# A two-layer MoE block and a two-layer FFN block on one core: the branch around the general path moved in front of the last group's third product

## The chip, the cores and the metric

The kernel runs on one core of one Trainium2 chip. The metric is device time in microseconds (us), here a median of several executions. A profile is one execution taken by the hardware profiler. The core's engines each work through their own queue of instructions in order: TensorE (PE; PEld are its weight loads), VectorE (DVE), ScalarE (ACT), GpSimd (POOL) and SyncE (SP), whose queue issues all loads here. They wait for each other by semaphores.

## The reference, cut to what matters

Two blocks run one after the other on 256 tokens of width 1024. The first has two layers of mixer and mixture of experts (MoE); the second has two layers of FFN, mixer, FFN. The change is in the MoE, which runs once per layer of the first block, and at its seam with what comes next:

```python
def run_block(args):                 # for each block of 128 assigned tokens
    tok, g, e = args
    xb = h2[tok]
    y = (jax.nn.silu(xb @ w1[e]) * (xb @ w3[e])) @ w2[e]
    return y * g[:, None]
...
    x = x + g2 * ffn                 # ffn: the sum of the experts' outputs of a token
```

Each token goes to two of sixteen experts. After the MoE of layer 0 comes `h = rms_norm(x, ...) * (1 + sc1) + sh1` and `proj = h @ in_w` of the odd mixer; after that of layer 1 comes `rms_norm_2(x, ...)` and `h @ w_gate` of the first FFN of the second block. So the stage behind needs the complete x.

## The kernel before, in words

The MoE packs the sixteen experts into seven groups of two or four experts (GROUPS), each of at most 128 rows of tokens in all, so that a group's tokens stand on the 128 partitions. For a group there are three products: the first with w1 and the second with w3 (line 1100, `up`), and the third with w2 (line 1119, `down`). Between them ScalarE applies silu (line 1162), VectorE multiplies by the second product and the gate (line 1169, tile hm), TensorE transposes hm (line 1106) and ScalarE copies the transposed tile out of PSUM (line 1108, tile tf), which is the third product's stationary operand. Behind it `weigh` scales by g2 (line 1128, tile yg) and splits the result into two parts (lines 301 and 303, tile yp), and `combine` multiplies by the transposed one-hot matrix ohT (lines 1136 and 1137) and adds to x (line 1138). The third product and the combine of a group run during the first two products of the next one. At the end of the loop the last group's third product (the function `finish`) and its combine stand alone.

An expert may receive more tokens than its place in a group holds. For those there is a general path (`overflow`, line 1208 on): a flag is loaded from SBUF into a register of each engine (line 1210), each engine compares and branches (line 1211, `tc.If`), and the body handles two blocks of 64 tokens at a time, up to four times. With the inputs measured the flag is zero, and the body is jumped over. At the join behind the body each engine waits until what it had issued before the branch is done, and then raises its semaphores by what the body would have raised them; SyncE waits for all its loads there.

Weights come in loads of 1 MB (line 266, tile raw, ten buffers; some as two halves through line 279 into the buffers wH and wL). They are issued by SyncE in program order, each when its buffer is free. For the dense products a load is split into two tiles of half the mantissa: ScalarE rounds it into wH (line 301), and VectorE or GpSimd writes the rest into wL (line 303). `ahead_of` runs at the end of the MoE: for the next stage's first two loads (`unit`, od_in in layer 0, the first FFN's gate weights in layer 1), it issues the load alone ("raw", layer 0) or the load and the split (False, layer 1).

The order of instructions on each engine is not the source's. The tile framework places each instruction by its own estimates, within what dependences and buffers allow, so a split of line 301 that the source writes in the next stage can stand ahead of the branch. What order results is shown below for the places that matter.

The next stage begins with `take` for each half of x: squares for the norm (line 448 on ScalarE, 450 on VectorE), and in layer 1 transposes of x (line 492) and their split into xTH and xTL (lines 495 and 496), which the FFN's products read (lines 321 to 323). In layer 0 x is first normed (xn, lines 464 and 465), then transposed (line 476) and split into hH and hL (lines 609 and 610) for the products of lines 562 to 564.

## Time and profile before

| | us |
|---|---|
| median of 3 runs | 1807.15 |
| lowest, highest | 1804.95, 1808.47 |
| the profiled execution's own time | 1807.92 |
| its span, first to last instruction | 1805.7 |
| TensorE busy in it | 1715.2 (95%) |
| VectorE, ScalarE, GpSimd busy | 904.5, 719.0, 96.2 |
| mean granted clock of TensorE, of full speed | 0.982 |

The span lies 2.2 us below the execution's own time. TensorE is busy for 95% of it, so the places of interest are those where it isn't. Two of them are the ends of the two MoE layers, at 439 to 461 us and at 805 to 835 us of the span, where the last group's third product and combine are done, the branch is passed, and the next stage's input is made. In timelines a row that ends in "[8.95 <-PEq L1211]" was preceded by 8.95 us of idle time on its engine, which ended with what stands behind the arrow; a "q" marks an engine's sequencer, which runs branches and semaphore waits.

### The profile page before, as it was taken

The numbers are of one execution on the slowest core, as the hardware profiler recorded it, in microseconds if no ns is written. First come the engines' busy times: TensorE is split into PE (matmuls) and PEld (weight loads), VectorE is DVE, ScalarE is ACT, GpSimd is POOL, SyncE is SP. The second block draws the span as 40 slices with busy tenths as digits, with TensorE's granted clock in tenths as the row PEclk, the third lists the DMA queues.
The fourth block names the chain that finished last, engine by engine and source line by source line (L and its number), as shares of the span: only waits on it lengthen the run. The fifth ranks groups of instructions, "written<-read, shape, count | busy, mean of one in ns | idle before, by whom it ended". The sixth has DMA issues, their size and how long they took to land.

```text
span 1805.7 us, 23867 instructions
## 1 busy us (share of the span) xinstructions
PE 1715.2 (95%) x9320; PEld 1202.5 (67%) x9320; DVE 904.5 (50%) x1570; ACT 719.0 (40%) x1100; POOL 96.2 (5%) x138
## 2 busy tenths in 40 slices
PE   6899999998899999997999999999999999999998
PEld 4765633333766433335888888888888888888886
DVE  3893632213657412125555665555465546655554
ACT  2434411111473211104444666544354436664442
POOL 0580000000100000000000000000000000000000
PEclk9899999999899999998999999999999999999999
DMA  9946699999977999997655642654655555426530
GB/s 365 354 165 256 247 404 418 417 415 381 339 281 267 356 412 417 416 411 271 198 187 180 198 158 94 209 182 169 194 180 185 186 187 203 141 94 210 186 117 24
DMA packets 148652, 454.81 MB, mean 252 GB/s; under 512 B 8608, under 2 KB 18992, under 8 KB 130608
## 3 DMA queue, kind: packets, MB, share of 16 engines
q1 hardware_dynamic: 148528, 453.16, 68.1%
q8 instruction: 78, 1.28, 0.3%
q14 instruction: 46, 0.38, 0.1%
HBM read 452.07 MB, written 1.05 MB: 251 GB/s over the span
## 4 chain that ended last, share of the span: by engine, by line
PE 53%; ACT 1%; issue 0%; DVE 0%; POOL 0%; DVEq 0%; POOLq 0%; ACTq 0%
PE acc L321 16%; PE acc L322 16%; PE acc L323 16%; PE tp L1293 1%; PE acc L1446 1%; PE tp L492 1%; PE acc L1356 1%; PE tp L1440 0%; PE tp L1410 0%; ACT wH L301 0%; PE acc L1385 0%; PE acc L1350 0%; ACT t L448 0%; PE acc L1351 0%; PE acc L1352 0%
## 5 line engine op out<-in xcount | busy, mean ns | idle before, releaser
L303 DVE TENSOR_TENSOR wL<-raw,wH 128x1024 fp32r<-128x1024 f32 x369 | 450.5, 1226 | 407.0 <-ACT wH L301 406.4
L301 ACT ACTIVATE wH<-raw 128x1024 fp32r<-128x1024 f32 x372 | 391.1, 1059 | 425.6 <-PE acc L323 393.4
L321 PE MATMUL acc<-wH,xTH 128*128 128x512 f32 (+1 forms) x928 | 353.0, 381 | 0.1
L323 PE MATMUL acc<-wH,xTL 128*128 128x512 f32 (+1 forms) x928 | 347.8, 377 | 2.4 <-DVE xTL L496 2.4
L322 PE MATMUL acc<-wL,xTH 128*128 128x512 f32 (+1 forms) x928 | 348.7, 377 | 0.0
L323 PEld LDWEIGHTS acc<-wH,xTL 128*128 128x128 f32 x928 | 174.4, 188 | 37.4 <-DVE xTL L496 3.7
L1100 PE MATMUL acc<-raw,xg 128*32 128x512 f32 (+1 forms) x1088 | 195.2, 596 | 3.8 <-DMA raw<-in_ex_w_dram 3.8
L321 PEld LDWEIGHTS acc<-wH,xTH 128*128 128x128 f32 x928 | 174.8, 188 | 32.1 <-ACT xTH L495 1.0
L322 PEld LDWEIGHTS acc<-wL,xTH 128*128 128x128 f32 x928 | 174.8, 188 | 32.1
L322 PE MATMUL acc<-wL,tH 128*128 128x512 f32 x352 | 139.2, 395 | 0.0
L321 PE MATMUL acc<-wH,tH 128*128 128x512 f32 x352 | 138.4, 393 | 0.0
L323 PE MATMUL acc<-wH,tL 128*128 128x512 f32 x352 | 137.4, 390 | 0.0
L1100 PEld LDWEIGHTS acc<-raw,xg 128*32 128x32 f32 (+1 forms) x1088 | 53.7, 120 | 115.1 <-issue 105.0
L1119 PE MATMUL acc<-raw,tf 128*64 128x512 f32 (+1 forms) x320 | 86.0, 599 | 1.1 <-DMA raw<-in_ex_w_dram 1.1
L365 PE MATMUL acc<-raw,condb 128*32 128x256 f32 x768 | 72.4, 494 | 9.9 <-DMA raw<-in_mod_w_dram 9.9
L562 PE MATMUL acc<-hH,wH 128*128 128x256 f32 x256 | 76.3, 298 | 5.7 <-ACT wH L301 5.7
L1169 DVE SCALAR_TENSOR_TENSOR hm<-acc,gg,hm 128x512 f32<-128x512 f32 x14 | 15.4, 1102 | 128.9 <-PE acc L1100 128.9
L335 POOL TENSOR_TENSOR rs<-ms,mhalf 128x1 f32<-128x1 f32 x22 | 12.1, 553 | 1252.9 <-DVE ms L334 1238.8
L1128 DVE TENSOR_TENSOR yg<-acc,g 128x512 f32<-128x512 f32 x28 | 19.2, 691 | 114.0 <-PE acc L1119 100.2
L321 PEld LDWEIGHTS acc<-wH,tH 128*128 128x128 f32 x352 | 66.1, 188 | 14.9
L323 PEld LDWEIGHTS acc<-wH,tL 128*128 128x128 f32 x352 | 66.1, 188 | 14.3
L563 PE MATMUL acc<-hL,wH 128*128 128x256 f32 x256 | 74.5, 292 | 0.8 <-DVE hL L610 0.8
(366 smaller groups left out, 2218.3 us busy)
## 6 DMA issues: line engine op xcount, KB each, us to landing
raw<-in_ex_w_dram SPq DMA_DIRECT2D x140, 1024.0 KB, 15.0
raw<-in_ffn_w_gate_dram SPq DMA_DIRECT2D x44, 1024.0 KB, 5.1
raw<-in_ffn_w_up_dram SPq DMA_DIRECT2D x44, 1024.0 KB, 5.1
raw<-in_ffn_w_down_dram SPq DMA_DIRECT2D x44, 1024.0 KB, 4.8
raw<-in_mod_w_dram SPq DMA_DIRECT2D x64, 512.0 KB, 7.9
rawwH<-in_ex_w_dram SPq DMA_DIRECT2D x52, 512.0 KB, 13.8
rawwL<-in_ex_w_dram SPq DMA_DIRECT2D x52, 512.0 KB, 12.6
raw<-in_w_in_dram SPq DMA_DIRECT2D x20, 1024.0 KB, 5.1
```

The lines of the kernel that those rows point to most:

```text
L301: S.activation(H, src, AF.Copy)
L303: eng.tensor_tensor(L, src, H.bitcast(F32), op=OP.subtract)
L321: TE.matmul(o, aH, bH, start=start, stop=False)
L322: TE.matmul(o, aH, bL, start=False, stop=False)
L323: return TE.matmul(o, aL, bH, start=False, stop=stop)
L365: TE.matmul(ps[32 * i:32 * i + 32, :], condb[:, k, :], quarter(raw[:, k % 2], i), start=k == 0, stop=k == 7)
L492: TE.transpose(ps[:, j, :], src[:, j * P:(j + 1) * P], ident)
L562: TE.matmul(o, ws[kk][0][:, cs], hH[:, k, :], start=k == 0 and c % 2 == 0, stop=False)
L563: TE.matmul(o, ws[kk][0][:, cs], hL[:, k, :], start=False, stop=False)
L1100: TE.matmul(ps[c:c + w, :], xg[:, k, c:c + w], ws[e][j], start=k == 0, stop=k == 7)
L1119: TE.matmul(y[h][c:c + w, :], tf[:, k, c:c + w], ws[e][j][:, half(h)], start=k == 0, stop=k == 3)
L1128: V.tensor_mul(yg, y[h], g2[:, half(h)])
```

## The change

At the end of the MoE's loop, the combine of the group before the last now comes first; then the loads of the last group's w2 are issued, then `ahead_of` and the branch, and only behind the branch stand the last group's transposed tile, its third product and its combine (`finish`). As the last group's tiles now have to outlive the general path, that has tiles of its own: `hmo` for hm, one buffer `one` of 128x512 for the weights (two of 128x1024 before, kept; now each use loads a half anew), and ohT has five buffers in place of four. In layer 1 `ahead_of` only loads, as in layer 0; the splits are then made where the first FFN asks for them, which gives wL of its first two loads to GpSimd (`FLEAD = 2`). The lines behind the first edit move by one (1211 becomes 1212, 301 becomes 302).

```diff
--- before.py
+++ after.py
@@ -283,15 +283,16 @@
     class Singly:
 
 
-        def __init__(self, ap, pl):
-            self.ap, self.pl, self.held = ap, pl, {}
-
-        def __getitem__(self, j):
-            if j not in self.held:
-                v = self.pl.tile([P, 1024], F32, name="one", bufs=2)[:, :self.ap.shape[2]]
-                nc.sync.dma_start(v, self.ap[:, j, :])
-                self.held[j] = v
-            return self.held[j]
+        def __init__(self, ap, pl, j=None):
+            self.ap, self.pl, self.j = ap, pl, j
+
+        def __getitem__(self, at):
+            if self.j is None and self.ap.shape[2] > 512:
+                return type(self)(self.ap, self.pl, at)
+            j, cols_ = (at, slice(0, 512)) if self.j is None else (self.j, at[1])
+            v = self.pl.tile([P, 512], F32, name="one", bufs=1)
+            nc.sync.dma_start(v, self.ap[:, j, cols_])
+            return v
 
     def after(ins):
         return tc.issue_after(ins.ins) if ins else ExitStack()
@@ -1060,7 +1061,7 @@
                 for t in range(2):
                     for i in range(n):
                         TE.transpose(pt[:, t, tok(i)], oh[:, t, tok(i)], identr)
-                ohT = [px.tile([P, 2, P], F32R, name="ohT", bufs=4) for _ in range(n)]
+                ohT = [px.tile([P, 2, P], F32R, name="ohT", bufs=5) for _ in range(n)]
                 for i in range(n):
                     S.activation(ohT[i], pt[:, :, tok(i)].bitcast(F32), AF.Copy)
                 return [(ohT[i], xg[:, :, tok(i)]) for i in range(n)]
@@ -1156,9 +1157,9 @@
 
                 return ws_of
 
-            def gated_(h1):
-
-                hm = px.tile([P, 4, P], F32, name="hm")
+            def gated_(h1, name="hm", **kw):
+
+                hm = px.tile([P, 4, P], F32, name=name, **kw)
                 S.activation(by_row(hm), rows_in(h1), AF.Silu)
                 return hm
 
@@ -1231,7 +1232,7 @@
                                              min_val=0, max_val=15) for s in range(2)]
                         dyn = lambda w, j: lambda hf: [Singly(rows_of(w, n_, hf, j), px) for n_ in n2]
                         tiles_ = ((0, 64, 0), (64, 64, 1))
-                        hm = gated_(up(dyn(w1, 4), xg, tiles_))
+                        hm = gated_(up(dyn(w1, 4), xg, tiles_), "hmo", bufs=1)
                         times(hm, up(dyn(w3, 4), xg, tiles_), gg)
                         combine(*weigh(down(dyn(w2, 2), turn(hm, acc), tiles_)), ohT)
                         if i < 3:
@@ -1272,12 +1273,14 @@
                 if not n:
                     blocks_of()
                 pend = (n, ohT, tiles_)
-            tf = turn(hm)
             combine(*done.pop())
-            finish(pend, tf)
+            for hf in range(2):
+                weights(pend[0], 2)(hf, True)
+            ahead_of()
+
+            overflow()
+            finish(pend, turn(hm))
             combine(*done.pop())
-            ahead_of()
-            overflow()
 
 
     def ffn(nx, wg, wu, wd, nxt, lead=0):
@@ -1520,7 +1523,7 @@
                 def ahead_of():
 
                     for hf in range(2):
-                        unit(*((first_ffn, 0) if layer else (od_in, D)), hf, False if layer else "raw")
+                        unit(*((first_ffn, 0) if layer else (od_in, D)), hf, "raw")
 
                 moe(layer, nm, rt, g2, [lambda: mod_rows(layer, 5, g2)], routed_f, ahead_of)
                 routed.close()
```

**ScalarE at the end of layer 0.** The rows of before, from the last group's yp and tf to the branch and the first row behind it; DMAHW1 and its like are the semaphores of eight lanes that the loads take in turn.

```order
L301 ACTIVATE yp<-yg 128x512 [waits DVE_49,Activation_49]
L1108 ACTIVATE tf<-tp 128x512 [waits PE_49]
L301 ACTIVATE yp<-yg 128x512 [waits DVE_49]
L301 ACTIVATE yp<-yg 128x512 [waits DVE_49,Activation_49]
L301 ACTIVATE yp<-yg 128x512 [waits DVE_49]
L301 ACTIVATE wH<-raw 128x1024 [waits DMAHW5_49,DMAHW7_49,DMAHW3_49,DMAHW1_49]
L301 ACTIVATE wH<-raw 128x1024
L1210 TENSOR_LOAD flagi [waits DVE_49]
L1211 COMPARE_AND_BRANCH
...
L1211 UNCONDITIONAL_BRANCH [waits Activation_49,Activation_sequencer_49]
L448 ACTIVATE t_4354,ss_4352<-x 128x512 [waits DVE_49]
L448 ACTIVATE t_4356,ss_4352<-x 128x512 [waits DVE_49]
```

The same place now:

```order
L302 ACTIVATE yp<-yg 128x512 [waits DVE_49,Activation_49]
L302 ACTIVATE yp<-yg 128x512 [waits DVE_49]
L302 ACTIVATE wH<-raw 128x1024 [waits DMAHW5_49,DMAHW7_49,DMAHW3_49,DMAHW1_49]
L302 ACTIVATE wH<-raw 128x1024
L1211 TENSOR_LOAD flagi [waits DVE_49]
L1212 COMPARE_AND_BRANCH
...
L1212 UNCONDITIONAL_BRANCH [waits Activation_49,Activation_sequencer_49]
L1109 ACTIVATE tf<-tp 128x512 [waits PE_49,Activation_49]
L302 ACTIVATE wH<-raw 128x1024 [waits DMAHW3_49,DMAHW5_49,DMAHW2_49,PE_49]
L302 ACTIVATE wH<-raw 128x1024 [waits DMAHW7_49,PE_49]
L302 ACTIVATE yp<-yg 128x512 [waits DVE_49,Activation_49]
L302 ACTIVATE yp<-yg 128x512 [waits DVE_49]
```

Row tf (line 1108, now 1109) has moved behind the branch, and behind the two rows wH<-raw that split the first load of od_in and wait for its lane, DMAHW1. Two more splits stand ahead of the last yp. Layer 1 reads the same, with the gate weights for od_in.

**TensorE at the end of layer 1.** Before, from the last of the combine of the group before the last to the first transposes of x:

```order
L1136 MATMUL acc<-yp,ohT 128x512 [waits PE_49]
L1137 MATMUL acc<-yp,ohT 128x512
L1119 MATMUL acc<-raw,tf 64x512 [waits DMAHW3_49,PE_49]
L1119 MATMUL acc<-raw,tf 64x512 [waits PE_49]
...
L1136 MATMUL acc<-yp,ohT 128x512
L1137 MATMUL acc<-yp,ohT 128x512
L1210 TENSOR_LOAD flagi [waits DVE_49]
L1211 COMPARE_AND_BRANCH
...
L1211 UNCONDITIONAL_BRANCH [waits PE_49,PE_sequencer_49]
L492 MATMUL tp<-cst,x 128x128 [waits DVE_49]
L492 MATMUL tp<-cst,x 128x128 x3
```

Now:

```order
L1137 MATMUL acc<-yp,ohT 128x512 [waits PE_49]
L1138 MATMUL acc<-yp,ohT 128x512
L1211 TENSOR_LOAD flagi [waits DVE_49]
L1212 COMPARE_AND_BRANCH
...
L1212 UNCONDITIONAL_BRANCH [waits PE_49,PE_sequencer_49]
L1120 MATMUL acc<-raw,tf 64x512 [waits DMAHW3_49,DVE_49,Activation_49]
L1120 MATMUL acc<-raw,tf 64x512 [waits DMAHW4_49]
L1120 MATMUL acc<-raw,tf 64x512 [waits DVE_49,PE_49]
...
L1137 MATMUL acc<-yp,ohT 128x512
L1138 MATMUL acc<-yp,ohT 128x512
L493 MATMUL tp<-cst,x 128x128 [waits DVE_49]
L493 MATMUL tp<-cst,x 128x128 x3
```

The third product (raw, rawwH and rawwL with tf) and the last combine have moved behind the branch, whose rows now follow the combine of the group before the last.

**VectorE at the end of layer 1.** Before, around the branch:

```order
L303 TENSOR_TENSOR yp<-yg,yp 128x512 [waits Activation_49] x2
L1138 TENSOR_TENSOR x<-x,acc 128x512 [waits PE_49] x2
L1138 TENSOR_TENSOR x<-x,acc 128x512
L1138 TENSOR_TENSOR x<-x,acc 128x512 [waits PE_49]
L303 TENSOR_TENSOR wL<-raw,wH 128x1024 [waits DMAHW2_49,DMAHW4_49,DMAHW1_49,DMAHW6_49,DMAHW0_49,Activation_49]
L1210 TENSOR_LOAD flagi [waits DVE_49]
L1211 COMPARE_AND_BRANCH
...
L1211 UNCONDITIONAL_BRANCH [waits DVE_49,DVE_sequencer_49]
L303 TENSOR_TENSOR wL<-raw,wH 128x1024 [waits DMAHW2_49,Activation_49]
L303 TENSOR_TENSOR wL<-raw,wH 128x1024 [waits DMAHW4_49,DMAHW6_49,DMAHW2_49,Activation_49]
L303 TENSOR_TENSOR wL<-raw,wH 128x1024 [waits DMAHW0_49,Activation_49]
L496 SCALAR_TENSOR_TENSOR xTL<-tp,vec,xTH 128x128 [waits PE_49]
```

Now:

```order
L1139 TENSOR_TENSOR x<-x,acc 128x512 [waits PE_49] x2
L1139 TENSOR_TENSOR x<-x,acc 128x512
L1139 TENSOR_TENSOR x<-x,acc 128x512 [waits PE_49]
L1211 TENSOR_LOAD flagi [waits DVE_49]
L1212 COMPARE_AND_BRANCH
...
L1212 UNCONDITIONAL_BRANCH [waits DVE_49,DVE_sequencer_49]
L1129 TENSOR_TENSOR yg<-acc,g_93 128x512 [waits DVE_49,PE_49,Activation_49] x2
L304 TENSOR_TENSOR yp<-yg,yp 128x512 [waits Activation_49] x2
L1139 TENSOR_TENSOR x<-x,acc 128x512 [waits PE_49] x2
...
L1139 TENSOR_TENSOR x<-x,acc 128x512 [waits PE_49]
L497 SCALAR_TENSOR_TENSOR xTL<-tp,vec,xTH 128x128 [waits Activation_49] x2
L455 TENSOR_TENSOR ss<-ss_8216 128x1
```

The four rows wL<-raw have left VectorE at this place; four such rows stand on GpSimd now, one ahead of its branch and three behind it.

## Rows read from the trace of the kernel before

**Rows 1.** The page, part 1: busy us (share of the span) and instructions by engine.

```profile
PE 1715.2 (95%) x9320; PEld 1202.5 (67%) x9320; DVE 904.5 (50%) x1570; ACT 719.0 (40%) x1100; POOL 96.2 (5%) x138
```

**Rows 2.** Timeline, end of layer 0: start, us, engine, line, operation, [idle before it <- releaser].

```profile
435.83 0.58 ACT L1108 ACTIVATE tf<-tp 128x512 f32<-128x512 f32 x1
...
438.60 3.66 PE L1119 MATMUL acc<-raw,tf 128*64 128x512 f32 x16
...
447.62 1.99 ACT L301 ACTIVATE wH<-raw 128x1024 fp32r<-128x1024 f32 x2
...
449.44 1.88 DVE L1138 TENSOR_TENSOR x<-x,acc 128x512 f32<-128x512 f32 x3 [0.23 <-PE acc L1137]
...
451.57 0.63 ACT L448 ACTIVATE t<-x 128x512 f32<-128x512 f32 x1 [1.96 <-DVEq L1211]
...
455.33 2.33 PE L476 MATMUL tp<-cst,xn 128*128 128x128 f32 x8 [5.07 <-DVE xn L464]
...
458.10 1.22 DVE L303 TENSOR_TENSOR wL<-raw,wH 128x1024 fp32r<-128x1024 f32 x1
...
461.26 0.58 PE L563 MATMUL acc<-hL,wH 128*128 128x256 f32 x1 [0.76 <-DVE hL L610]
```

**Rows 3.** Line 1211, the branch in layer 0: shortest/median/longest ns, first to last start.

```profile
L1211 DVEq EVENT_SEMAPHORE  x2: 21/21/21, 451.5 to 451.6; - x2
L1211 PEldq EVENT_SEMAPHORE  x2: 51/51/51, 452.6 to 452.8; - x2
...
L1211 PEldq COMPARE_BRANCH  x1: 3402/3402/3402, 449.1 to 449.1; - x1
```

**Rows 4.** Line 1211, SyncE's waits alone, at 444 to 447 and 809 to 812 us.

```profile
L1211 SPq EVENT_SEMAPHORE  x1: 17/17/17, 445.2 to 445.2; - x1
...
L1211 SPq EVENT_SEMAPHORE  x1: 17/17/17, 810.5 to 810.5; - x1
```

**Rows 5.** Timeline, end of layer 1.

```profile
801.79 0.58 ACT L1108 ACTIVATE tf<-tp 128x512 f32<-128x512 f32 x1
...
804.56 3.66 PE L1119 MATMUL acc<-raw,tf 128*64 128x512 f32 x16
...
813.58 1.99 ACT L301 ACTIVATE wH<-raw 128x1024 fp32r<-128x1024 f32 x2
...
814.49 2.58 DVE L1138 TENSOR_TENSOR x<-x,acc 128x512 f32<-128x512 f32 x4
...
824.56 1.94 PE L492 MATMUL tp<-cst,x 128*128 128x128 f32 x8 [8.95 <-PEq L1211]
...
827.03 2.36 DVE L303 TENSOR_TENSOR wL<-raw,wH 128x1024 fp32r<-128x1024 f32 x2 [7.27 <-ACT wH L301]
...
829.31 0.60 DVE L496 SCALAR_TENSOR_TENSOR xTL<-tp,vec,xTH 128x128 fp32r<-128x128 f32 x2
...
834.94 0.50 PE L321 MATMUL acc<-wH,xTH 128*128 128x512 f32 x1
```

**Rows 6.** Line 1211, the branch in layer 1, TensorE.

```profile
L1211 PEldq EVENT_SEMAPHORE  x2: 51/51/51, 818.4 to 824.5; - x2
...
L1211 PEldq COMPARE_BRANCH  x1: 3394/3394/3394, 814.9 to 814.9; - x1
```

**Rows 7.** Windows: length, busy us (instructions) by engine, granted clock of TensorE, DMA share, GB/s.

```profile
461.30:465.90 4.60, 4.60 (x22) 4.60 (x23) 2.71 (x8) 1.61 (x5) 0.00 (x0) 0.50 1.03 408
465.90:470.00 4.10, 4.10 (x36) 4.10 (x36) 1.22 (x1) 2.10 (x2) 0.00 (x0) 1.00 1.02 401
804.55:811.70 7.15, 7.14 (x33) 2.54 (x32) 1.53 (x3) 0.00 (x0) 0.00 (x0) 1.00 1.04 388
815.65:824.50 8.85, 0.00 (x0) 0.00 (x0) 3.79 (x5) 0.72 (x2) 0.00 (x0) 0.79 0.74 257
820.80:827.70 6.90, 2.80 (x10) 2.10 (x10) 0.67 (x1) 2.01 (x3) 0.00 (x0) 0.51 1.05 391
...
500.00:525.00 25.00, 25.00 (x186) 18.94 (x185) 9.69 (x17) 17.78 (x34) 0.00 (x0) 1.00 0.85 312
```

More of the change, by code (lines that the diff above doesn't have):

```diff
@@ L1274, in moe @@
                 pend = (n, ohT, tiles_)
-            tf = turn(hm)
             combine(*done.pop())
-            finish(pend, tf)
-            combine(*done.pop())
+            for hf in range(2):
+                weights(pend[0], 2)(hf, True)
             ahead_of()
             overflow()
+            finish(pend, turn(hm))
+            combine(*done.pop())
     def ffn(nx, wg, wu, wd, nxt, lead=0):
```

## The prediction

> **What bounds the kernel now.** I read the page first: TensorE is busy for 95% of the span [rows 1], so what this change can win or lose lies in the few places where TensorE stands still. Two of them are the seams behind the two MoE layers, and there the timeline and the instructions of the branch's line say what it stands still for. The seams differ, and this difference carries the whole forecast.
>
> In layer 0 the last group's third product begins at 438.60, its combine is added to x until 451.3, and TensorE's next work, transposes of xn, begins at 455.33 after a wait for VectorE [rows 2]. TensorE's compare-and-branch takes 3.40 us, from 449.1, and its last wait at the join is passed at 452.8 [rows 3]. So in layer 0 TensorE is through its branch 2.5 us before its input is there: the branch costs TensorE nothing here. In layer 1 the first half of x is complete at about 815.1 (the first of four additions that begin at 814.49 and take 2.58 in all), but TensorE's transposes of it begin only at 824.56, and the row says that its own sequencer ended the idle time, at line 1211 [rows 5]. The compare takes 3.39 us from 814.9, and between the two waits of the join, 818.4 and 824.5, TensorE loses another 6.1 us [rows 6]. TensorE waits in the joins for its own earlier work alone, and that was done at 815.6 in layer 1, so I take the 3.4 and the 6.1 us for the fetching of code behind a jump. That is 9.4 us (824.56 less 815.1) on the path, in one layer of two.
>
> What is lost at either seam reaches the end in full: x is needed whole by the next stage, and behind the seams TensorE runs without a gap (25.00 of 25 us busy at 500 to 525, with the loads at 0.85 of their engines, [rows 7]), so no slack absorbs it.
>
> **What the change removes and adds.** The branch now stands ahead of the last group's third product on every engine. On TensorE that puts the 3.4 us of the compare right behind the combine of the group before, at 438.6 and 804.5, and a second code wait beside or behind work. What decides is ScalarE. The third product needs tf, which ScalarE wrote at 435.83 and 801.79, before the product began [rows 2, 5]. In the changed order tf stands behind ScalarE's branch, and ahead of that branch stand two splits wH<-raw of the next stage's first load. They wait for this load to land, and an engine works in order, so tf waits with them.
>
> When does it land? SyncE's waits in the join of before tell it: the lane of that load is the second it waits for, and that wait ends at 445.2 in layer 0 and at 810.5 in layer 1 [rows 4]. The loads ahead of it in SyncE's queue are the same in both kernels, so these times stand. The hold of layer 0: 445.2, two splits 1.99 [rows 2], the two waits of a join 0.1 to 0.2 (VectorE's lie 0.1 apart, [rows 3]), tf 0.58, so the third product begins at about 448.0 instead of 438.6: **9.4 us later**. Layer 1: 810.5, 1.99, 0.15 and 0.58 give 813.4 instead of 804.56: **8.8 us later** [rows 4, 5]. TensorE's own branch, begun at about 438.4 and 804.4, is over at 442 and 808 and hidden in that; its second code wait, by the spacing of layer 1 over some 9.5 us after the compare began, at 448 and 814, is hidden too or nearly so.
>
> [...]
>
> [...] The third product takes 7.15 us at the full clock [rows 7]. After the hold its first four us or so run at the lower one, which costs half of them, **2.0 us per layer**. Bounds: 0, if the clock doesn't fall in time, and 3.5, if it stays low for 6.9 us as from 820.8 to 827.7.
>
> Behind the third product the changed order is better than that of before.
> - Layer 0: one wL of 1.22 us [rows 2] now stands on VectorE between yg and yp of the last group; TensorE has the other half of that combine to do meanwhile, so 0 to 1.2, taken 0.6. Against it, ScalarE's first square (451.57) waited for VectorE's join, though additions to x had been ending for 2 us [rows 2, 3]; two of three squares of 0.6 now fall beside the additions, 1.2 won (0 to 1.3). And the wL at 458.10 that stood ahead of the first hL, for which TensorE waited until 461.26 [rows 2], is gone from there: 1.1 won (0 to 1.2).
> - Layer 1: the 9.4 us of the branch are won. In the 10.4 us from the first transposes (824.56) to gapless products (834.94), two wL of 2.36 in all stood on VectorE ahead of the first xTL at 829.31 [rows 5]; these splits are on GpSimd now, which is busy for 5% of the span [rows 1]. 2.4 won from them, and 0.9 because squares are done beside the additions: 3.3 (0 to 5).
> - SyncE issues one load fewer ahead of the branch and passes the join when two loads have landed instead of three, some 2.6 us earlier; the bytes are the same, and TensorE is late. I cost it at nothing; the cover is TensorE's own delay.
> - The tiles of the general path cost nothing, since it is jumped over.
>
> The sum: layer 0 is 9.4 + 2.0 + 0.6 - 1.2 - 1.1 = +9.7; layer 1 is 8.8 + 2.0 - 9.4 - 3.3 = -1.9. Together **+7.8 us** against the profiled execution's 1807.92 (span 1805.7 and 2.2 around it): 1815.7. The median of before is 0.8 below that execution, so 1814.9, in round numbers 1815. The ends: with every cost at its top and no relief +9.4 + 3.5 + 1.2 + 8.8 + 3.5 - 9.4 = +17.0, about 1824; with no loss by the clock and all relief 9.4 - 2.5 + 8.8 - 9.4 - 5 = +1.3, about 1808.5.
>
> **The rivals.**
> *ScalarE isn't held.* If the first load had landed by the time the last yp of the group before is split, about 437 and 803, the splits would run at once, and the third product would only wait for TensorE's compare: 3.4 - 2.3 + 0.6 in layer 0, 3.4 - 9.4 - 3.3 in layer 1, -7.6 in all, about 1799.5, faster than before. It decides where a load lands 8 us earlier than [rows 4] say; the loads are at 388 GB/s and 1.04 of their engines in that stretch [rows 7], and I see nothing that would hurry one.
> *The load lands a little earlier.* The third load of the next stage is no longer in flight behind the first two. If the sixteen engines had been serving it beside them, the first would land up to one load earlier, 1 MB at 388 GB/s [rows 7] or 2.7 us, in both layers: +7.8 - 5.4 = +2.4, about 1809.5, which is no change that can be measured. For it speaks that the loads overlap; against it, that they land one after the other.
> *A second code wait behind the hold.* The 6.1 us between TensorE's two waits [rows 6] appear in layer 1 and not in layer 0 [rows 3], so it depends on where the jump lands in the code. If it hits the third product or the combine after the hold, one layer pays up to 6.1 us more: about 1821. [...]
>
> **How the numbers follow.** A measurement of this kernel can tell about 0.2%, 3.6 us, from no change. Chances: the forecast 0.72, ScalarE not held 0.06, the load earlier 0.12, the second code wait 0.10. Faster by over 0.2% (below 1803.5) is the first rival, 0.06. Within 0.2% are the second rival and the forecast's own low end, 0.12 + 0.03 = 0.15. The rest, 0.79, is slower. The range from 1808.5 to 1821 holds the forecast with most of its bounds and the middle two; it leaves out the fast case and the sums in which all goes badly.
>
> **What would show it.** In the changed profile tf of the last group (line 1109) should start at about 447.3 and 812.7, right behind two splits wH<-raw that a load released; TensorE's idle time of 9 us ahead of the third product (line 1120) should be put down to ScalarE's tf; that product should take 9 us instead of 7.15, half of it at the lower clock. In layer 1 the first transposes of x should follow the additions to x without a wait for line 1212, at about 826, and the stretch from them to gapless products should be 7 us instead of 10.4. If tf starts before 442 or 808, the hold is wrong and with it the sign; if TensorE's idle time is put down to its own sequencer, the code wait is.

## The result: slower by 0.7%, and the profile after

The changed kernel takes 1819.72 us (median of 4 runs, 1817.36 to 1820.11), the kernel before 1806.47 (median of 4, one more than in the table above, 1804.95 to 1808.47): a ratio of 1.007, with a 95% interval from 1.0058 to 1.0083. The forecast was 1815, with a range from 1808.5 to 1821. The profiled execution took 1820.11 us with a span of 1818.3, so 12.6 us of span have come in.

The page after, its head and part 1: TensorE's busy time answers to [rows 1] and has hardly moved (1714.2 for 1715.2); what came in is idle time.

```profile
span 1818.3 us, 23880 instructions
...
PE 1714.2 (94%) x9320; PEld 1199.9 (66%) x9320; DVE 905.6 (50%) x1566; ACT 720.7 (40%) x1100; POOL 105.9 (6%) x142
```

The timeline after, end of layer 0, answers to [rows 2]:

```profile
445.71 2.00 ACT L302 ACTIVATE wH<-raw 128x1024 fp32r<-128x1024 f32 x2 [9.31 <-SPq L1212]
447.97 0.60 ACT L1109 ACTIVATE tf<-tp 128x512 f32<-128x512 f32 x1 [0.26 <-ACTq L1212]
...
448.62 5.76 PE L1120 MATMUL acc<-raw,tf 128*64 128x512 f32 x16 [10.33 <-ACT tf L1109]
...
457.94 2.38 POOL L304 TENSOR_TENSOR wL<-raw,wH 128x1024 fp32r<-128x1024 f32 x1 [6.45 <-ACT wH L302]
458.56 2.84 DVE L304 TENSOR_TENSOR wL<-raw,wH 128x1024 fp32r<-128x1024 f32 x1
462.06 1.44 PE L1138 MATMUL acc<-yp,ohT 128*128 128x512 f32 x4 [1.73 <-DVE yp L304]
467.08 2.33 PE L477 MATMUL tp<-cst,xn 128*128 128x128 f32 x8 [3.59 <-DVE xn L465]
```

Line 1212, the branch, at the same place (shortest/median/longest ns, first to last start), answers to [rows 3]:

```profile
L1212 PEldq EVENT_SEMAPHORE  x2: 51/51/51, 444.1 to 444.2; - x2
L1212 ACTq EVENT_SEMAPHORE  x2: 17/17/17, 447.7 to 447.8; - x2
...
L1212 PEldq COMPARE_BRANCH  x1: 6268/6268/6268, 437.8 to 437.8; - x1
...
L1212 ACTq COMPARE_BRANCH  x1: 50/50/50, 446.2 to 446.2; - x1
```

ScalarE's two splits start when the load has landed, at 445.71; only then does ScalarE come to its branch (446.2), and behind that to tf (447.97). TensorE is through its own branch at 444.2 and has stood still for 10.33 us when the third product begins. The end of layer 1, answering to [rows 5]:

```profile
822.19 2.00 ACT L302 ACTIVATE wH<-raw 128x1024 fp32r<-128x1024 f32 x2 [7.34 <-SPq L1212]
824.45 0.60 ACT L1109 ACTIVATE tf<-tp 128x512 f32<-128x512 f32 x1 [0.26 <-ACTq L1212]
...
825.10 5.25 PE L1120 MATMUL acc<-raw,tf 128*64 128x512 f32 x16 [8.38 <-ACT tf L1109]
...
834.01 5.13 POOL L304 TENSOR_TENSOR wL<-raw,wH 128x1024 fp32r<-128x1024 f32 x2 [5.98 <-PE acc L1120]
834.66 5.03 DVE L304 TENSOR_TENSOR yp<-yg,yp 128x512 fp32r<-128x512 f32 x2
841.18 1.91 PE L493 MATMUL tp<-cst,x 128*128 128x128 f32 x8
```

It is the same picture, with one thing that layer 0 hasn't: VectorE's two yp take 5.03 us, where before they took 0.68 each (1.29 in all), while GpSimd writes wL. The row of before:

```profile
813.16 1.29 DVE L303 TENSOR_TENSOR yp<-yg,yp 128x512 fp32r<-128x512 f32 x2 [0.16 <-ACT yp L301]
```

The transposes of x then follow without a wait for the branch.

Where the 12.6 us lie shows best when the same work is looked up in both traces and the starts are subtracted:

| work | start before | later by |
|---|---|---|
| combine of the group before the last, layer 0 | 435.98 | -0.3 |
| third product of the last group | 438.60 | 10.0 |
| x complete (end of VectorE's last addition) | 451.32 | 13.8 |
| first transposes of xn | 455.33 | 11.8 |
| a product of the next stage, full clock from here | 465.89 | 9.3 |
| the next mixer, low clock ahead of it | 543.48 | 8.5 |
| the same, 4 us on | 547.83 | 11.1 |
| combine of the group before the last, layer 1 | 801.93 | 12.2 |
| third product of the last group | 804.56 | 20.5 |
| x complete | 817.07 | 25.4 |
| first transposes of x | 824.56 | 16.6 |
| products of the first FFN | 834.49 | 13.0 |
| the same, 37 us on | 871.38 | 12.5 |

So layer 0's seam costs 9.6 us, the stretch between the seams 2.9, and layer 1's seam 0.3. Each column is one execution. How far such a figure can be trusted shows in pad248, further down, which does the same work as the kernel before up to layer 1's branch: between 461 and 466 us its starts move by 2.0 us against those of before, which ran at a granted clock of 0.50 there [rows 7]; that its low clock ended earlier is inferred from these starts.

### The profile page after: what moved, and what is told of

The parts are those of the page before. It is cut to its first block, busy times and chain, and to the rows that moved or that the text cites. A ratio compares the mean times of both kernels' runs of the same rounds, so it can differ in the third digit from the quotient of the medians.

```text
span 1818.3 us, 23880 instructions
## 1 busy us (share of the span) xinstructions
PE 1714.2 (94%) x9320; PEld 1199.9 (66%) x9320; DVE 905.6 (50%) x1566; ACT 720.7 (40%) x1100; POOL 105.9 (6%) x142
## 4 chain that ended last, share of the span: by engine, by line
PE 53%; DVE 1%; ACT 0%; issue 0%; POOL 0%; DVEq 0%; POOLq 0%; ACTq 0%
PE acc L322 16%; PE acc L324 16%; PE acc L323 16%; PE tp L1296 1%; PE tp L493 1%; PE acc L1449 1%; PE acc L1359 1%; PE acc L1120 0%; PE tp L1443 0%; DVE yp L304 0%; PE tp L1413 0%; PE acc L1388 0%; PE acc L1353 0%; PE acc L1354 0%; ACT wH L302 0%
## 5 line engine op out<-in xcount | busy, mean ns | idle before, releaser
L366 PE MATMUL acc<-raw,condb 128*32 128x256 f32 x768 | 70.8, 486 | 10.3 <-DMA raw<-in_mod_w_dram 10.3
L323 PEld LDWEIGHTS acc<-wL,tH 128*128 128x128 f32 x352 | 66.2, 188 | 13.0
L565 PE MATMUL acc<-hH,wL 128*128 128x256 f32 x256 | 74.2, 292 | 0.5 <-DVE wL L304 0.5
## 6 DMA issues: line engine op xcount, KB each, us to landing
rawwH<-in_ex_w_dram SPq DMA_DIRECT2D x52, 512.0 KB, 13.8
rawwL<-in_ex_w_dram SPq DMA_DIRECT2D x52, 512.0 KB, 12.6
```

The lines of the kernel that those rows point to most:

```text
L323: TE.matmul(o, aH, bL, start=False, stop=False)
L366: TE.matmul(ps[32 * i:32 * i + 32, :], condb[:, k, :], quarter(raw[:, k % 2], i), start=k == 0, stop=k == 7)
L565: TE.matmul(o, ws[kk][1][:, cs], hH[:, k, :], start=False, stop=k == 7 and c % 2 == 1)
```

## The experiments

All times are medians (of 10 executions for only0, only1, raw_only, pad1, own and pad248, of 4 for the others) against runs of the kernel before on the same chip. Where the text says how late a kernel is at a place, the start of the same work is compared in its profile and in that of before.

| kernel | us | before | ratio, 95% interval |
|---|---|---|---|
| tf_first | 1819.75 | 1806.33 | 1.0068, 1.0051 to 1.0085 |
| split_late | 1813.97 | 1805.84 | 1.0043, 1.0026 to 1.0059 |
| only0 | 1808.42 | 1806.33 | 1.0014, 1.0004 to 1.0025 |
| only1 | 1808.97 | 1806.33 | 1.0018, 1.0008 to 1.0027 |
| no_raw | 1818.40 | 1806.33 | 1.0074, 1.0057 to 1.0090 |
| raw_only | 1803.13 | 1805.84 | 0.9980, 0.9967 to 0.9993 |
| pad1 | 1802.00 | 1805.84 | 0.9976, 0.9966 to 0.9986 |
| swap | 1797.31 | 1808.10 | 0.9943, 0.9926 to 0.9960 |
| own | 1800.41 | 1808.10 | 0.9958, 0.9945 to 0.9971 |
| pad248 | 1805.28 | 1806.38 | 0.9992, 0.9981 to 1.0003 |
| pad1_raw | 1797.12 | 1805.84 | 0.9940, 0.9923 to 0.9958 |
| own_raw | 1797.13 | 1806.38 | 0.9941, 0.9921 to 0.9961 |

### What holds the third product: tf, or ScalarE's branch

tf_first is the changed kernel with tf written ahead of the branch (and a tile of its own for the general path's):

```diff
+            tf = turn(hm)
             ahead_of()
 
             overflow()
-            finish(pend, turn(hm))
+            finish(pend, tf)
```

> The changed kernel with one thing more: the last group's transposes of hm and their copy tf are written ahead of the branch (the general path's tf has a tile of its own), while the third product stays behind it. In the changed kernel's trace ScalarE's branch waits for a load until 445.71 and tf starts at 447.97, so that the third product starts at 448.62 (layer 0) and 825.10 (layer 1), while TensorE itself is through its branch at 444.2 and 822.5. Theory (ScalarE's tf is held behind splits that wait for a load): tf starts near 435.5 in layer 0 without a wait for a load, the third product starts at TensorE's own end of the branch, near 444.3, that is 4.3 us earlier than in the changed kernel, and 2.5 us earlier in layer 1: about 1819.7 - 6.8 = 1813, between 1811 and 1815. Rival one (the hold costs nothing that TensorE's code wait would not cost as well): 1819.7. Rival two (without the hold the moved branch is worth what it was meant to bring): below 1804.

Nothing was won: 1819.75. The timeline of tf_first, end of layer 0:

```profile
437.15 0.58 ACT L1109 ACTIVATE tf<-tp 128x512 f32<-128x512 f32 x1
...
449.12 6.27 PE L1120 MATMUL acc<-raw,tf 128*64 128x512 f32 x16 [9.12 <-ACTq L1212]
```

tf is there at 437.7, and the product still begins at 449.12. What ended TensorE's wait is now ScalarE's sequencer at the branch's line. The kernel's text offers one thing that can tie the product to it: the PSUM banks (acc) that the product writes are those that ScalarE reads in the general path, for silu and for that path's own tf. Which buffer it is, no profile says. So tf was only one of two bonds to the same point, ScalarE's join. My theory, 1813, named the wrong bond, and the time is that of rival one; the point, ScalarE's branch behind two splits, was still to be tried. split_late leaves tf where the change put it and holds the splits back:

```diff
-                S.activation(tf, pt, AF.Copy)
+                hold[0] = S.activation(tf, pt, AF.Copy)
...
+        begin = begin if w is None else hold[0]     # in loadw: splits of loads made ahead
```

> The changed kernel, but the splits of the next stage's first loads are held back until tf is issued, so that on ScalarE no split stands ahead of the branch; loads, branch and third product stay where the change put them. The kernel with tf ahead of the branch had tf written at 437.15 and its third product still began at 449.12, behind a wait for ScalarE's sequencer at the branch's line: so it is ScalarE's join that TensorE waits for, not tf alone. New theory: with ScalarE at its branch at about 436.5, TensorE waits for its own code alone: third product near 444.3 instead of 448.6 in layer 0 and 2.5 us earlier in layer 1, 1819.7 - 6.8 = 1813, between 1811 and 1815. Rival (some third thing holds the product, or what is won is lost again behind it): 1818 to 1821.

The waits of line 1213 in split_late at layer 0's join, and its timeline of ScalarE and TensorE at the two seams (its lines stand one further):

```profile
L1213 ACTq EVENT_SEMAPHORE  x2: 17/17/17, 436.5 to 436.6; - x2
L1213 PEldq EVENT_SEMAPHORE  x2: 51/51/51, 444.2 to 444.4; - x2
...
444.36 0.60 ACT L1110 ACTIVATE tf<-tp 128x512 f32<-128x512 f32 x1 [7.93 <-PEq L1213]
445.01 5.42 PE L1121 MATMUL acc<-raw,tf 128*64 128x512 f32 x16 [6.71 <-ACT tf L1110]
...
817.81 5.05 PE L1121 MATMUL acc<-raw,tf 128*64 128x512 f32 x16 [6.38 <-ACT tf L1110]
```

1813.97 against 1819.72: 5.7 won, 6.8 expected. So the splits ahead of ScalarE's branch are what the third product waited for last, and that was worth 5.7 of the 13.3 us. The missing us is in the row of tf: ScalarE passes its join at 436.5, and tf then waits for TensorE's join (444.2 to 444.4), so the product starts 0.7 after that and not with it. What is left of the loss, 8.1 us by the medians and 5.5 by the profiles' spans, goes with the moved branch itself: TensorE stands still for 6.71 and 6.38 us ahead of the product, since its jump takes 6.35 and 6.19 us there. By the starts of the same work layer 0's seam costs 5.6 us now, the stretch between the seams 1.6, and layer 1's seam gives 1.9 back.

### Which seam costs what

only0 and only1 make the change at the end of one layer, with the order of before at the other. Both keep the rest of the change, the general path's own tiles and layer 1's `ahead_of` that only loads:

```diff
+            if layer == 0:                          # only1: layer == 1
                 combine(*done.pop())
                 ...                                 # the changed order
+            else:
+                tf = turn(hm)
+                combine(*done.pop())
+                finish(pend, tf)
+                combine(*done.pop())
+                ahead_of()
+                overflow()
```

> The moved branch in layer 0 alone; in layer 1 the order of before (third product and combine, then ahead_of with the load alone, then the branch). In the changed trace TensorE's work is 9.3 us late at the end of layer 0's seam, 12.2 late at the start of layer 1's seam and 12.5 late behind it. Theory (the seams add up, layer 0 is the whole loss): layer 0's seam 9 to 10 us late as in the changed kernel; at layer 1's seam the GpSimd splits are in place, so some 2 to 3 us are won back there: about 1806.5 + 9.5 + 1 - 3 = 1814, between 1812 and 1818. There is one thing by the way: layer 1's jump of TensorE lands four instructions further in the code than before; if the 6.1 us between TensorE's two waits [rows 6] hang on where the jump lands, they may be gone, which would give about 1808. Rival (the loss is in layer 1's seam): 1806.

> The moved branch in layer 1 alone; layer 0 has the order of before. Theory: no delay at layer 0's seam (transposes of xn near 455.3); in layer 1 the hold as in the changed kernel (third product 8.4 us later than before), the branch's 9.4 us gone from behind it, net +0.3: 1806.5 to 1808. Of the changed kernel's 12.5 us, 2.9 arise between the two seams; if layer 0's delay brings them (by where the low clock falls), they are absent here; rival (they come with the general path's own tiles or the code as such): 1809.5. Rival two (layer 1's seam carries the loss): 1814 or more.

Layer 0 came out as expected: in only0 its seam puts TensorE 9 to 10 us late, in only1 it costs nothing. only1, at 1808.97, lies over its range of 1806.5 to 1808. Its profile is 3.3 us early already at 207 us, ahead of the seams; counted from the start of layer 1's seam that costs 2.1, with the third product 9.6 late, for the expected 0.3. And of the 2.9 us between the seams, most of one piece (1.6) is there too, with no delay at layer 0's seam, so that delay isn't what brings it. But only0 was at 1808.4, not 1814: at layer 1's seam 11.3 us of lateness shrink to 1.9. This is line 1212 there:

```profile
L1212 PEldq EVENT_SEMAPHORE  x2: 51/51/51, 830.2 to 830.4; - x2
...
L1212 PEldq COMPARE_BRANCH  x1: 3894/3894/3894, 826.3 to 826.3; - x1
```

TensorE's two waits, 6.1 us apart before [rows 6], are 0.2 apart, in a join that is the same but for four instructions of code ahead of it. That part of the 9.4 us in layer 1 hasn't to do with where the branch stands. Of the 9.5 us that only0 wins back at this seam, 5.4 are won up to the first transposes of x and 4.1 from them to the products; these 4.1 are the split's part, next.

### GpSimd and VectorE

no_raw is the changed kernel with layer 1's splits made by ahead_of as before, raw_only the kernel before with only that edit of the change:

```diff
-unit(*((first_ffn, 0) if layer else (od_in, D)), hf, False if layer else "raw")
+unit(*((first_ffn, 0) if layer else (od_in, D)), hf, "raw")    # raw_only; no_raw is the reverse
```

> The changed kernel with layer 1's ahead_of as before (it makes the splits too), so that wL of the first FFN's first two loads stands on VectorE and not on GpSimd. In the changed trace the last group's two yp on VectorE take 2.26 and 2.84 us instead of 0.68 while GpSimd writes wL (834.01 to 839.14), and TensorE's combine waits for them. Theory (GpSimd's tensor_tensor and VectorE's with both operands in SBUF take turns): yp takes 0.68 us each again; against it two wL of 1.2 us now stand on VectorE between yg and yp of that group, so x is complete some 1.3 us earlier: about 1818.4, between 1816.5 and 1820. Rival (GpSimd's splits are a gain as the prediction had it, 2.4 us of 3.3): 1822 or more, with yp as long as in the changed kernel or longer.

> The kernel before with the one edit that layer 1's ahead_of only loads; the splits are made where the first FFN asks, wL on GpSimd. Theory (the prediction's 2.4 + 0.9 us): from the first transposes of x (824.56) to gapless products about 7 us instead of 10.4, yp and the additions to x unhurt, since GpSimd's splits fall behind them: 1806.3 - 3.4 = 1803, between 1801.5 and 1804.5. Rival (GpSimd's splits stretch VectorE's steps by as much as they take off its queue): 1806.3.

The timeline of no_raw, VectorE at the end of layer 1:

```profile
833.04 2.36 DVE L304 TENSOR_TENSOR wL<-raw,wH 128x1024 fp32r<-128x1024 f32 x2
835.32 0.68 DVE L304 TENSOR_TENSOR yp<-yg,yp 128x512 fp32r<-128x512 f32 x1
...
837.31 0.69 DVE L304 TENSOR_TENSOR yp<-yg,yp 128x512 fp32r<-128x512 f32 x1
```

yp is back at 0.68, and what is won there is spent on the two wL ahead of it: 1818.40, 1.3 less than the changed kernel and within its scatter; layer 1's seam alone costs 0.6 us in its profile, and 0.3 in the changed kernel's. From the first transposes of x to the products no_raw wins the same 4.2 us, with GpSimd idle. So this gain comes from the splits no longer standing between these transposes and xTL, whichever engine makes them. In raw_only, where the branch stands as before, GpSimd's splits are a gain of 2.7 us, and none of VectorE's steps to x is stretched:

```profile
812.86 2.58 DVE L1138 TENSOR_TENSOR x<-x,acc 128x512 f32<-128x512 f32 x4
...
813.12 4.67 POOL L303 TENSOR_TENSOR wL<-raw,wH 128x1024 fp32r<-128x1024 f32 x2 [240.76 <-ACT wH L301]
```

Four additions x<-x,acc take 2.58 us here as in [rows 5], right beside GpSimd's split. acc lies in PSUM, so they read one operand from SBUF; yp reads two. TensorE's two waits at raw_only's join are still 6.3 us apart, so it isn't this edit that closed the gap in only0:

```profile
L1211 PEldq EVENT_SEMAPHORE  x2: 51/51/51, 817.0 to 823.3; - x2
```

### The second wait for code

pad1 makes layer 1's general path, which is jumped over, 128 TensorE instructions longer (17 times each transpose in place of one), swap makes layer 0's 64 longer, pad248 layer 1's 248. What is executed is the kernel before.

```diff
-                for k in range(4):
-                    TE.transpose(pt[:, k, :], hm[:, k, :], ident)
+                for k in range(4):
+                    for _ in range(reps):           # 1, but in layer 1's general path 17 (pad1)
+                        TE.transpose(pt[:, k, :], hm[:, k, :], ident)
```

own is the kernel before with the change's tiles for the general path alone (the diff's first, second, third and fourth pieces).

> The kernel before, with one thing more: in layer 1's general path, which is jumped over, the four transposes stand 17 times, so that TensorE's jump lands 128 instructions further in its code. Nothing that is executed changes. In the kernel with the changed branch in layer 0 alone that jump landed four instructions further than before, and TensorE's two waits at the join were 0.2 us apart instead of 6.1. Theory (the 6.1 us [rows 6] are a second fetch of code, because the jump lands at the end of a stretch of code that is fetched at once): the two waits 0.2 us apart, transposes of x at about 818.5 instead of 824.56, 6.1 us won: 1800.4, between 1799 and 1803. Rival (that wait has another cause, and the four instructions were a coincidence): 1806.3.

> The kernel before, with layer 0's general path (jumped over) 64 TensorE instructions longer. Nothing that is executed changes, but by the compiled code layer 0's jump now lands where layer 1's landed, counted in pieces of 256 instructions (instruction 214 of one), and layer 1's lands 64 further (22 of the next). Theory (the second wait hangs on that position alone): layer 0 gets a wait of about 6 us between TensorE's two waits at the join, 452.6 to 458.7, so that the transposes of xn start at about 458.8 instead of 455.33 and 3.4 us are lost there, since 2.5 us are covered; layer 1 loses its 6.1 us wait: 1805.8 + 3.4 - 5.5 = 1803.7, between 1802 and 1805.5, and the trace shows both. Rival (something in layer 1 itself makes the wait): layer 0 as before, layer 1 as before, 1806.

> The kernel before with nothing but the general path's own tiles (hmo, one, ohT with five buffers); the branch and ahead_of as before. By the prediction this costs nothing: 1806, layer 0's and layer 1's seams as before. One thing can upset that: the general path becomes one TensorE instruction longer per layer, so that layer 1's jump lands two instructions further, 216 of a piece of 256 instead of 214 (218 was past the second wait, 214 was not). If 216 is past it too, TensorE's 6.1 us go and the time is about 1800.5, for a reason that has nothing to do with tiles.

> The kernel before, with layer 1's general path (jumped over) 248 TensorE instructions longer: 256 less 8, so that the jump lands eight instructions ahead of where it landed before, counted in pieces of 256. So far TensorE's second wait at layer 1's join came 6.1 us late with its position in such a piece at 213, and 0.2 us behind the first with it at 215, 217, 85 and 21; with layer 0's jump moved to 213 nothing was late there. Theory (in layer 1 a fetched piece ends between 212 and 213, and the next one arrives 6 us later): now both waits (204, 205) pass together at about 818.4, three transposes of x (207 to 212) run, and the fourth stops until about 824.5; the time is that of before less half a us, 1805 to 1808, in spite of the longer path. Rival (any move of the code takes the wait away, as pad1 and own did): 1800 to 1802, transposes without a gap.

(The texts count in two ways: 214 or 216 is the last instruction of the join, and the second wait stands one ahead of it, at 213 or 215.)

pad1 and own did as expected: by their profiles 5.9 us are won at layer 1's seam in each, by the medians 3.8 and 7.7 in all. TensorE's waits in pad1's layer 1:

```profile
L1212 PEldq EVENT_SEMAPHORE  x2: 51/51/51, 817.9 to 818.0; - x2
...
L1212 PEldq COMPARE_BRANCH  x1: 3374/3374/3374, 814.5 to 814.5; - x1
```

swap missed in layer 0, which has no wait there, and in its time, 1797.31 for 1802 to 1805.5; in layer 1 it did as expected. Its two pairs of waits:

```profile
L1212 PEldq EVENT_SEMAPHORE  x2: 51/51/51, 448.8 to 449.0; - x2
```

```profile
L1212 PEldq EVENT_SEMAPHORE  x2: 51/51/51, 813.3 to 813.5; - x2
```

So the same count doesn't bring a second wait in both layers; at which count layer 0 would have one was not tried. (Of the 11.4 us by which the span of swap's profile is shorter, 3.7 stand ahead of layer 0's branch, where the work is as before and no cause is known, and 5.9 at layer 1's seam.) The sharp one is pad248, TensorE in layer 1's join and behind it:

```profile
L1212 PEldq EVENT_SEMAPHORE  x2: 51/51/51, 818.5 to 818.7; - x2
...
818.81 0.52 PE L492 MATMUL tp<-cst,x 128*128 128x128 f32 x3 [3.48 <-PEq L1212]
824.34 1.23 PE L492 MATMUL tp<-cst,x 128*128 128x128 f32 x5 [5.02 <-issue]
```

Both waits pass at 818.5 and 818.7, three transposes run, and the fourth stops for 5.02 us with nothing to wait for that the profile shows: eight instructions earlier in the code, the gap stands eight instructions later in the work. The time is that of before. So the 6.1 us of [rows 6] hang on a place in TensorE's code and not on any wait or instruction. The DMA queues of the kernel before fit a fetch of code there: the one that the page calls instruction (q8) moved 1.28 MB in 78 packets, 16 KB each. From 850 to 1750 us it had 35 packets while TensorE did 8901 matmuls and weight loads, 254 to a packet, near the 256 by which the texts count. One packet runs from 821.9 to 822.9 us, within the stop that ends at 824.5. That TensorE waited for this packet is a reading of these times; the view doesn't say whose code it is.

### Both gains, with the branch left where it was

pad1_raw joins pad1 and raw_only, own_raw joins own and raw_only.

> Both of the last two in one kernel: the jump of layer 1 lands 128 instructions further, and layer 1's ahead_of only loads. Theory (the two gains add up, since the code wait ends where the transposes begin and the splits cost behind them): 1806.3 - 6.1 - 3.4 = 1796.8, between 1795 and 1799.5. Rival (the next stage's loads are late as soon as TensorE is early): 1800 or more.

> The kernel before with two parts of the change that leave the branch where it was: the general path's own tiles (which by chance move layer 1's jump past the second wait) and layer 1's ahead_of with the load alone. Theory: as with the padded path, 6.1 + 3 us won, 1797, between 1795 and 1799.5. Rival (the gains don't add up): 1800 or more.

1797.12 and 1797.13: about 9 us under the kernel before and 22 under the changed one. So two small parts of the change are worth 0.5%, and the part it is named for costs more than that. How much can be told: only0 and only1 are own_raw with the branch moved in one layer, and the changed kernel is own_raw with it moved in both. Against the kernel before on the same chip own_raw stands at -9.3 us, only0 at +2.1, only1 at +2.6 and the changed kernel at +13.3. A moved branch costs 11.3 us in layer 0, 11.9 in layer 1 and 22.5 in both, so that the two nearly add up. TensorE in own_raw, layer 1:

```profile
819.09 1.94 PE L493 MATMUL tp<-cst,x 128*128 128x128 f32 x8 [2.91 <-PEq L1212]
```

## Why the prediction was right, and where it was off

The sign and the range held, and so did the mechanism that it named for the loss, but this mechanism is only part of the loss. The forecast was +7.8 us by its sum; the profile shows +12.6 and the medians +13.3. By the steps:

| step | forecast | profile |
|---|---|---|
| layer 0: third product held | 9.4 | 10.3 |
| layer 0: low clock in it | 2.0 | 2.1, of which 1.3 come back |
| layer 0: wL between yg and yp | 0.6 | 1.7 |
| layer 0: squares beside the additions | -1.2 | -2.0 |
| layer 0: wL gone from ahead of hL | -1.1 | -1.2 |
| layer 0 | 9.7 | 9.6 |
| between the seams | 0 | 2.9 |
| layer 1: third product held | 8.8 | 8.4 |
| layer 1: low clock in it | 2.0 | 1.6 |
| layer 1: yp beside GpSimd | no term | 3.2 |
| layer 1: branch gone from behind x | -9.4 | -8.8 |
| layer 1: from transposes to products | -3.3 | -4.2 |
| layer 1 | -1.9 | 0.3 |

That layer 0 agrees to 0.1 us is in part luck: its steps are off by +0.9, -1.2 (the clock, with what comes back), +1.1, -0.8 and -0.1.

**The hold** was read rightly from SyncE's waits [rows 4]: 445.71 and tf at 447.97 for a forecast 445.2 and 447.3. (In layer 1 the forecast's own terms add up to 813.2 and not to 813.4, which changes nothing.) split_late shows that it is the last thing the product waits for, and that it is worth 5.7 of 13.3 us. Two things in its reason were too narrow. That tf stands behind the branch is not needed: tf_first, with tf at 437.15 and the time unchanged, shows a second bond to ScalarE's join that alone does the same. And the sign didn't hang on it: the prediction let TensorE's own branch be over at 442 and hidden, but its jump takes 6.27 us at the new place instead of 3.40, and without the hold the product is still 6.7 and 6.4 us late.

**The branch's 9.4 us** behind x were won as forecast (8.8). But 6.1 of them came with the place where the jump landed in the code, and pad1 and own win them with the branch where it was. So the credit was right against this kernel before, and not as a gain of the move.

**The low clock** cost what was forecast in the product: 16 matmuls in 5.6 and 5.1 us instead of 3.5. The 2.0 us per layer in the sum were the author's estimate, which no run shows; the runs showed 2.1 and 1.6. The window of layer 0's product after (columns as in [rows 7]) shows a granted clock of 0.77 on average, between the levels of 0.50 and 1.00:

```profile
448.60:457.80 9.20, 9.18 (x32) 2.65 (x32) 0.69 (x1) 1.67 (x2) 2.89 (x2) 0.77 0.85 295
```

That 1.3 us come back in layer 0 was overlooked: before, the dense products ran at the low level for 4.6 us from 461.3 [rows 7]; now they begin at 471.5, and the granted clock is 0.50 up to 473.3, for 1.8 us, and 0.98 in the 2 us behind. The other kernels with layer 0's branch moved win 1.3 to 1.8 us there. But pad248, with nothing changed at that seam, wins 2.0, so this step is not clear of chance.

**The step that failed** is layer 1's term of 3.3 us for the wL given to GpSimd, in that it was priced by GpSimd's 5% alone. The gain came (4.2, and as no_raw shows without GpSimd too), but GpSimd's splits run at the very time when VectorE splits yp, and yp then takes 2.26 and 2.84 us in place of 0.68: 3.2 us on the path. Tile yp after, VectorE's instructions at the end of layer 1:

```profile
L304 DVE TENSOR_TENSOR yp<-yg,yp x2: 2258/2550/2843, 834.7 to 836.8; 128x512 fp32r<-128x512 f32 x2
```

Layer 0's wL, 1.22 us in [rows 2], of which 0.6 were priced, took 2.84 beside GpSimd's split of 457.94 to 460.32. The trace shows the two engines in each other's way: yp ends 0.55 us after GpSimd's split does, both times, and GpSimd's second split, begun while the first yp was still under way, takes 2.80 us instead of 2.36. The additions with one operand in PSUM lose nothing in raw_only, 2.58 us for four as before. So the operands in SBUF are the reading that fits; what the two engines share there no view shows.

**Between the seams** 2.9 us were not forecast. The prediction took it that a loss passes on unchanged, as TensorE runs without a gap behind the seams, and read this from 500 to 525 us alone; just ahead of 541 there is a gap. The 2.9 us come in two pieces. At 543 to 548 us 2.7 are lost, after 0.8 had been won just ahead. Windows of that stretch, before and then after, where the same work comes 9 to 11 us later:

```profile
538.00:541.00 3.00, 0.72 (x7) 0.41 (x3) 2.74 (x9) 2.29 (x6) 0.00 (x0) 0.99 1.02 371
541.00:544.00 3.00, 2.69 (x7) 1.93 (x7) 3.00 (x5) 0.00 (x0) 0.00 (x0) 0.50 0.99 415
544.00:547.00 3.00, 2.33 (x10) 1.55 (x9) 3.00 (x8) 0.34 (x1) 0.00 (x0) 0.94 0.99 380
```

```profile
553.00:556.00 3.00, 1.70 (x4) 1.10 (x4) 3.00 (x8) 0.00 (x0) 0.00 (x0) 0.50 1.01 355
556.00:559.00 3.00, 3.00 (x9) 2.29 (x9) 2.61 (x7) 1.67 (x3) 0.00 (x0) 0.55 0.96 380
```

Both have a time at the lower of the two levels, but after, it lies later in the work and lasts through 3 us in which TensorE is busy throughout. The same loss of 2 us or more shows in the profiles of tf_first, split_late, only0, only1 and no_raw, one of 0.9 in own and pad248, and none in pad1, swap, raw_only, pad1_raw and own_raw. So it comes where the branch is moved in either layer, also where it is moved in layer 1 alone, which comes later; why the clock falls where it does stays open. The other piece, about 1 us in all between 548 and 692, I can't name.

**The rivals.** "ScalarE isn't held" was priced at 1799.5; split_late comes to the same by other means, and it took 1814. The rival's price was wrong, first because it took 3.4 us for TensorE's jump from a place with little traffic (a DMA share of 0.06 and 0.13). At the new place, with 1.03 and 0.96, it takes 6.27 and 6.23 us. It also had no term for the low clock, and split_late's product has it: 16 matmuls in 5.25 and 4.88 us instead of 3.5. For the forecast this did no harm, since the hold is longer still. "A second code wait behind the hold" had 1821, near the measured time, but it isn't what happened: TensorE's two waits at the join are 0.1 and 0.2 us apart, and the added time is in yp and between the seams. The load didn't land earlier: the splits that wait for it start at 445.71 for 445.2, and in layer 1 at 822.19, which is 810.0 for 810.5 when the 12.2 us of lateness are taken off.

## What to carry to other kernels

A branch that is jumped over is a meeting point: here work behind it that takes over operands or buffers waited for the joins of the engines that use them in the path, so before moving one look at what stands ahead of it on each engine, here two splits that wait for a load, and not only at the operand that was moved. A split given to idle GpSimd was free here only where VectorE wasn't doing work with two operands in SBUF at the same time: four additions kept their 2.58 us beside it, yp went from 0.68 to 2.26 and 2.84. And where an engine waits behind a jump with all its semaphores up, move the code by a few instructions before moving the branch: here that was worth 5.9 us at the seam, and came by chance with an edit that was to cost nothing.

## What the runs showed of the hardware

**A jump cost TensorE 3.3 to 3.9 us where little was loaded, and 6.2 to 6.3 us where loads filled the DMA engines.** The windows of the four jumps, before and after (DMA share is the last column but one):

```profile
449.00:452.40 3.40, 1.26 (x3) 0.44 (x2) 2.10 (x4) 1.44 (x4) 3.40 (x2) 0.50 0.06 20
814.90:818.30 3.40, 0.72 (x4) 0.23 (x2) 3.30 (x5) 0.67 (x1) 0.00 (x0) 1.00 0.13 30
```

```profile
437.80:444.10 6.30, 0.49 (x3) 0.06 (x1) 1.88 (x3) 0.00 (x0) 0.00 (x0) 0.89 1.03 387
816.00:822.30 6.30, 0.72 (x4) 0.25 (x2) 2.06 (x4) 0.11 (x1) 0.00 (x0) 0.94 0.96 356
```

0.06 and 0.13 of the engines with 3.40 and 3.39 us, 1.03 and 0.96 with 6.27 and 6.23. In all kernels with a moved branch the ten jumps that stand ahead of the product take 6.15 to 6.35 us, with a DMA share of 1.03 for only0's 6.28. Sixteen jumps that stand behind the last combine take 3.34 to 3.89, with 0.06 and 0.08 for swap's 3.34 and 3.50, and 0.31 for only0's 3.89. In the four windows one packet of q8 begins 1.0 us after the jump does in both of before, and 3.6 and 3.7 us after it in those of after, and takes 0.9 to 1.1 us. Place and traffic change together and traffic was not varied by itself, so that it is the cause is argued, not shown.

**Behind a jump, TensorE in layer 1 stopped once more at a fixed place in its code, until some 6 us after its first wait in the join.** The two waits are 6.1 us apart in the kernel before and 6.3 in raw_only. pad248 shows it with work around it: a stop of 5.02 us between two transposes. That a next piece of code arrives there is the reading that fits, with the one packet of q8 in that stop; the loads kept the DMA engines at 0.99 from 818.4 to 824.5 in the kernel before, and what the stop would be without them no run shows.
